# A decoder trunk on one core: value product behind the third head's q and k, gate products ahead of the z products, transposes one step later

## The chip, the cores and the metric

The kernel runs on one core of a Trainium2 chip. The metric is the device time of one launch in microseconds. Before the change three runs gave 2627.89, 2624.89 and 2626.27 us; their median is 2626.27 us.

## What is computed

Two layers of a hybrid decoder trunk over 512 tokens of width 1024, all in float32. Each layer is a half-step feed-forward block, a mixer and a second half-step feed-forward block; a last norm follows. The change touches the mixer only:

```python
proj = h @ w_in[l]
q, k, v, z, xbc, dt_raw, gate_sb, gate_ssm = jnp.split(proj, IN_SPLITS, axis=-1)
y_sb = stick_breaking_attention(q, k, v) @ w_branch_sb[l]              # 4 heads x 128
y_ssm = mamba2_mixer(z, xbc, dt_raw, ...) @ w_branch_ssm[l]            # 24 heads x 64, 8 groups
merged = jax.nn.sigmoid(gate_sb) * y_sb + jax.nn.sigmoid(gate_ssm) * y_ssm
x = x + merged @ w_out[l]
```

Inside `mamba2_mixer`, xbc goes through a causal convolution of four taps and silu and splits into x, b and c; a chunked scan over four chunks of 128 tokens gives y, which is multiplied with silu(z) and normalised by groups.

## The kernel before

Activations lie transposed, channels on the 128 partitions and the 512 tokens along the free axis. Every float32 operand of a product is kept as two parts, a rounded high part and the rest (`hhi` and `hlo` for the input h, `whi` and `wlo` for weights), and one product of a 128x128 weight block with 128x512 activations is three TensorE matmuls (`mm3`, lines 316 to 320). A weight unit is 128 output columns over 1024 inputs: one DMA of 512 KB into `wraw`, a ScalarE cast into `whi` (line 285) and a VectorE subtraction into `wlo` (line 287), two units ahead of use. A product over it is eight times `mm3`.

The order of the work on every engine is the order in which the program issues it. The main stream issues products. Beside it runs a list of generators (`spawn`): after each `mm3` of a product, `tick` lets every generator whose count has run out issue its next instructions. `yield n` in a generator means: go on n steps later. So a **step** is one `mm3` of the main stream, and the number in a yield sets how many matmuls TensorE has in front of it when it meets the generator's next instruction. TensorE takes matmuls in that order; when an operand is not there, everything behind it waits. `flush` runs the steps that are left without a product between them.

The products go round four PSUM banks of the pool `pmm` (trace name `mm`); attention's scores and the scan use `pa` (two banks), transposes and the heads' value products `ptr` (two banks, trace name `pt`). A product that writes the bank of the product four places before it needs that one read out.

Order of the mixer's products. `qkv_order` (line 105) gives q and k of heads 0 and 1, then v, then q and k of head 2, dt, and q and k of head 3. The first four are issued before the loop over the order: q0 and k0 into `pa`, q1 and k1 into two `mm` banks. During k1 the input h is replaced by its normed form, block by block (`swapped`, lines 352 to 359, `hhi` at 357 and `hlo` at 358). The four outputs q0 to k1 are scaled by the norm afterwards (`scaled`, trace name `raw`, lines 546 and 548) and split into `yt` pairs (lines 406 and 411); q and k of the later heads are split straight from PSUM. v and z are made token by token (`by_tokens`, line 877): four weight units, and in each of them all four token blocks c = 0 to 3, so all four `mm` banks are in use at once; c = 0 opens its bank at once, c = 3 opens the last one after six `mm3`. v has 512 columns, z 384, and a matmul of 384 columns takes less time. z of pair p has four units.

`attention` (line 906) runs as one generator for each head, one head at a time: scores of four key blocks (lines 929 to 943), suffix sums on TensorE and weights (lines 945 to 964, in buffers `dec`, `btok`, `cT` and `bT`, two of each, one pair for each head), and, when all weights and all of v are there (line 983), the value product into `pt` (lines 986 to 989). `opened` (line 995) holds the end of each convolution until all four heads and dt are done.

`group_steps` (line 62) orders the rest in four pairs p: b and c of two groups, three x blocks, z, and gate products (`gs`, `gm`) where a 1 or a true condition stands. `conv_block` (line 1001) reads a bank with one ScalarE and three VectorE instructions (lines 1009 and 1012), then takes tanh (1017) and one VectorE instruction (1024), yields 2, and transposes x and b on TensorE (`transposed`, line 854, trace line 859). Its two scratch tiles come from the rooms `raw` and `cv`, three of each. `sigma` (line 1214) reads a gate's bank with one tanh (1218). `z_part` (line 1050) reads z's banks (1067, 1069). `ssd_group` (line 1077) is the scan of one group, one group at a time; at its end the group's result `yn` (trace name `raw`, line 1193) and every second time `tail` (`acc`) are transposed after `yield 3`.

Of the kernel before, what the change touches and what calls it, by code (L numbers as in the profile page):

```python
# [19 lines left out]
NT = SEQ // P  # L20
# [3 lines left out]
SBH = 4  # L24
# [37 lines left out]
def group_steps():  # L62


    gates = iter([(t, m) for m in range(EARLY) for t in ("gs", "gm")])
    for p in range(GROUPS // 2):
        a, b = 2 * p, 2 * p + 1
        if p == 0:
            steps = [("z", p), ("b", a), 1, ("c", a), ("x", 0), 1, ("x", 1), ("x", 2), 1, ("b", b), ("c", b), 1]
        else:  # L70
            steps = [("b", a), ("c", a), 1, ("x", 3 * p), ("x", 3 * p + 1), ("z", p), ("x", 3 * p + 2), p < 3,
                     ("b", b), ("c", b), p < 2, p < 2]
            if p == 3:
                steps[2] = 0
        for step in steps:
            if step in (0, 1):
                if step:
                    yield next(gates)
            else:
                yield step  # L80
    yield from gates
    for m in range(EARLY, KB):
        yield "gs", m
        yield "gm", m


def conv_at(kind, i):

    if kind == "x":
        return OFF_X + i * P, i * TAPS  # L90
    at = (OFF_B, OFF_C)[kind == "c"] + i * P
    return at, (DIN // P + GROUPS * (kind == "c") + i) * TAPS
# [12 lines left out]
def qkv_order():  # L105


    yield from (("q", 0), ("k", 0), ("q", 1), ("k", 1))
    for u in range(NT):
        yield "v", u  # L110
    for h in range(2, SBH):
        yield from (("q", h), ("k", h))
        if h == SBH - 2:
            yield "dt", None


# [5 lines left out]
def unit_order(layer):  # L122
# [14 lines left out]
    for t, h in qkv_order():  # L137
        yield ((layer, "dt") if t == "dt" else (layer, t, h)), KB
    for kind, i in group_steps():
        if kind == "z":  # L140
            for u in range(NT):
                yield (layer, "z", i, u), 2 * 2 * GW // P
        else:
            yield (layer, kind, i), KB
# [22 lines left out]
class Builder:  # L167
# [833 lines left out]
    def conv_block(self, kind, i, ps):  # L1001


        nc, mp = self.nc, self.mp
        r = yield from self.take("raw")
        u = yield from self.take("cv")
        _, k0 = conv_at(kind, i)
        tap = [self.conv[:, k0 + j:k0 + j + 1] for j in range(TAPS)]
        nc.scalar.activation(u, ps, AF.Identity, scale=tap[KCONV - 1], bias=tap[KCONV])
        yield 2  # L1010
        for j in range(1, KCONV):
            nc.vector.scalar_tensor_tensor(u[:, j:], ps[:, :SEQ - j], tap[KCONV - 1 - j], u[:, j:],  # L1012
                                           op0=ALU.mult, op1=ALU.add)
            yield 1
        yield 1
        yield from self.opened()
        nc.scalar.activation(r, u, AF.Tanh)
        yield 1
        if self.cumb is None:
            self.load_cum(0)  # L1020
        dst = u
        if kind != "x":
            dst = self.ssm[i][kind] = self.t(mp, [P, SEQ], kind + "T")
        nc.vector.scalar_tensor_tensor(dst, r, 1.0, u, op0=ALU.add, op1=ALU.mult)
        yield 2
        if kind == "x":
            p, i = divmod(i, 3)
            pt = self.transposed(dst)
            yield 1
            for g in (2 * p, 2 * p + 1):  # L1030
                a, b = max(i * P, g % 2 * GW), min((i + 1) * P, (g % 2 + 1) * GW)
                if a < b:
                    if "x" not in self.ssm[g]:
                        while not self.room["xs"]:
                            yield 1
                        self.room["xs"] -= 1
                        self.ssm[g]["x"] = self.t(mp, [P, NT, GW], "xs", bufs=3)
                    nc.scalar.activation(self.ssm[g]["x"][:, :, a - g % 2 * GW:b - g % 2 * GW],
                                         pt[:, :, a - i * P:b - i * P], AF.Copy, scale=0.5)
                    self.ssm[g]["x", i] = True  # L1040
            yield 1
        elif kind == "b":
            pt = self.transposed(dst, NT - 1)
            yield 1
            tok = self.t(mp, [P, NT - 1, P], "btok")
            nc.scalar.copy(tok, pt)
            self.ssm[i]["btok"] = tok
        self.give("raw", "cv")
# [28 lines left out]
    def ssd_group(self, layer, g):  # L1077
# [120 lines left out]
        if g % 2:  # L1198
            todo.append((tail, 3 * (g // 2) + 2))
        for src, blk in todo:  # L1200
            yield 3
            pt = self.transposed(src.rearrange("p c d -> p (c d)")).rearrange("p c d -> p (c d)")
            if src is yn:
                self.give("raw")
            yield 1
            gain = par[:, G_SSM + blk:G_SSM + blk + 1]
            hi, lo = self.pair(self.yt, ("yt", "yt"))
            nc.scalar.activation(hi, pt, AF.Copy, scale=gain)
            yield 1
            nc.vector.scalar_tensor_tensor(lo, pt, gain, hi.bitcast(F32), op0=ALU.mult, op1=ALU.subtract)  # L1210
            self.y_ssm[blk] = (hi, lo)
# [31 lines left out]
    def mixer(self, layer):  # L1243
# [4 lines left out]
        self.hx = []  # L1248
        first = []
        order = list(qkv_order())  # L1250
        for i in range(4):
            while i == 3 and self.scaled_blocks < KB // 2:
# [4 lines left out]
        with ExitStack() as mix:  # L1257
# [20 lines left out]
            with tc.tile_pool(name=f"mp{layer}", bufs=2, reuse_waits="tile") as self.mp:  # L1278
# [23 lines left out]
                for kind, i in group_steps():  # L1302
                    if kind == "z":
                        self.by_tokens(partial(self.z_part, i), 2 * GW, layer, "z", i)
                    elif kind in ("gs", "gm"):
                        gates.setdefault(i, []).append(open_gate(kind, i))
                    else:
                        self.spawn(self.conv_block(kind, i, self.project(layer, kind, i)[0]))
# [197 lines left out]
```

## Time and profile before

| what | value |
|---|---|
| median of three runs | 2626.27 us |
| the profiled execution, its own time | 2627.45 us |
| its span, first to last instruction | 2625.5 us |
| mean granted TensorE clock | 0.997 |
| VectorE busy | 1748.9 us (67%) |
| ScalarE busy | 1280.8 us (49%) |
| GpSimd busy | 506.9 us (19%) |
| mixer of layer 0, first product of v to the last transposes | about 379 to 838 us |

The profile shows one execution. Times in it are microseconds from the first instruction. PE is TensorE, PEld its weight loads, DVE VectorE, ACT ScalarE, POOL GpSimd. A busy PE need not be at its peak: a matmul's record lasts longer than the distance to the next one, since they are pipelined. In the timeline a row gives start, duration, engine, line, operation, tiles as out<-in, form and count, and in brackets how long the engine was idle before it and which instruction ended that.

### The profile page before, as it was taken

The numbers are of one execution on the slowest core, as the hardware profiler recorded it, in microseconds if no ns is written. First come the engines' busy times: TensorE is split into PE (matmuls) and PEld (weight loads), VectorE is DVE, ScalarE is ACT, GpSimd is POOL, SyncE is SP. The second block draws the span as 40 slices with busy tenths as digits, with TensorE's granted clock in tenths as the row PEclk, the third lists the DMA queues.
The fourth block names the chain that finished last, engine by engine and source line by source line (L and its number), as shares of the span: only waits on it lengthen the run. The fifth ranks groups of instructions, "written<-read, shape, count | busy, mean of one in ns | idle before, by whom it ended". The sixth has DMA issues, their size and how long they took to land.

```text
span 2625.5 us, 38311 instructions
## 1 busy us (share of the span) xinstructions
PE 2588.9 (99%) x15122; PEld 2307.6 (88%) x15122; DVE 1748.9 (67%) x2362; ACT 1280.8 (49%) x2087; POOL 506.9 (19%) x629
## 2 busy tenths in 40 slices
PE   9999999999999999999999999999999999999998
PEld 7898978888888889899998989788888888899997
DVE  7575875565675478585885858656666744776766
ACT  6343556755554255353553535466555532543434
POOL 1120201133232003021120311012322310021210
PEclk9999999999999999999999999999999999999999
DMA  6465442333333555474554645323333335474642
GB/s 185 137 155 140 122 133 73 100 101 116 101 100 94 164 149 158 134 184 112 160 143 123 178 128 133 118 74 107 101 108 99 100 110 163 130 183 127 178 122 80
DMA packets 105157, 336.36 MB, mean 128 GB/s; under 512 B 12256, under 2 KB 15584, under 8 KB 104976
## 3 DMA queue, kind: packets, MB, share of 16 engines
q1 hardware_dynamic: 93168, 293.46, 35.8%
q0 software_dynamic: 10944, 39.85, 8.6%
q8 instruction: 119, 1.95, 0.3%
q10 hardware_dynamic: 864, 0.60, 0.1%
q14 instruction: 62, 0.51, 0.1%
HBM read 321.18 MB, written 12.68 MB: 127 GB/s over the span
## 4 chain that ended last, share of the span: by engine, by line
PE 90%; DVE 6%; ACT 2%; issue 1%; DMA 1%; POOL 0%; SPq 0%; DVEq 0%; ACTq 0%
PE mm L318 25%; PE mm L320 25%; PE mm L319 25%; PE pa L320 3%; PE pa L319 3%; PE pa L318 3%; DVE wlo L287 2%; PE pa L1142 1%; DVE cv L1012 1%; ACT whi L285 1%; PE pa L953 1%; PE pt L859 1%; PE pa L1144 1%; PE pt L1127 1%; PE pt L1125 0%
## 5 line engine op out<-in xcount | busy, mean ns | idle before, releaser
L285 ACT CAST whi<-wraw 128x1024 fp32r<-128x1024 f32 (+2 forms) x442 | 435.8, 986 | 601.7 <-PE mm L320 487.7
L287 DVE TENSOR_TENSOR wlo<-wraw,whi 128x1024 fp32r<-128x1024 f32 (+2 forms) x442 | 544.6, 1232 | 209.5 <-ACT whi L285 208.8
L318 PE MATMUL mm<-hhi,whi 128*128 128x512 f32 (+1 forms) x1600 | 575.0, 359 | 1.1 <-ACT hhi L505 1.1
L319 PE MATMUL mm<-hhi,wlo 128*128 128x512 f32 (+1 forms) x1600 | 559.9, 350 | 2.1 <-DVE wlo L287 2.1
L320 PE MATMUL mm<-hlo,whi 128*128 128x512 f32 (+1 forms) x1600 | 560.8, 351 | 0.1
L320 PEld LDWEIGHTS mm<-hlo,whi 128*128 128x128 f32 x1600 | 303.1, 189 | 40.9 <-DVE hlo L507 0.5
L319 PEld LDWEIGHTS mm<-hhi,wlo 128*128 128x128 f32 x1600 | 303.7, 190 | 39.1 <-DVE wlo L287 3.3
L318 PEld LDWEIGHTS mm<-hhi,whi 128*128 128x128 f32 x1600 | 303.6, 190 | 38.0 <-DVE z L1069 1.6
L622 POOL TENSOR_TENSOR g<-g,rs 128x512 f32<-128x512 f32 x76 | 132.7, 1746 | 736.0 <-DVE g L629 715.2
L318 PE MATMUL mm<-act,whi 128*128 128x512 f32 (+1 forms) x710 | 274.3, 386 | 0.0
L287 DVE TENSOR_TENSOR wlo<-s,whi 128x1024 fp32r<-128x1024 f32 x152 | 235.4, 1563 | 58.5 <-ACT whi L285 58.5
L319 PE MATMUL mm<-act,wlo 128*128 128x512 f32 (+1 forms) x710 | 274.1, 386 | 0.0
L320 PE MATMUL mm<-act,whi 128*128 128x512 f32 (+1 forms) x710 | 274.0, 386 | 0.0
L320 PE MATMUL mm<-tl,whi 128*128 128x256 f32 x912 | 258.6, 284 | 0.0
L319 PE MATMUL mm<-th,wlo 128*128 128x256 f32 x912 | 258.6, 284 | 0.0
L318 PE MATMUL mm<-th,whi 128*128 128x256 f32 x912 | 258.5, 283 | 0.0
L285 ACT CAST whi<-s 128x1024 fp32r<-128x1024 f32 x152 | 158.9, 1045 | 100.7 <-PE mm L320 59.0
L648 DVE SCALAR_TENSOR_TENSOR x<-mm,x 128x512 f32<-128x512 f32 x93 | 64.1, 690 | 196.1 <-PE mm L320 196.1
L319 PEld LDWEIGHTS mm<-th,wlo 128*128 128x128 f32 x912 | 175.3, 192 | 0.0
L318 PEld LDWEIGHTS mm<-th,whi 128*128 128x128 f32 x912 | 175.3, 192 | 0.0
L320 PEld LDWEIGHTS mm<-tl,whi 128*128 128x128 f32 x912 | 175.3, 192 | 0.0
L320 PEld LDWEIGHTS mm<-act,whi 128*128 128x128 f32 x710 | 133.5, 188 | 26.7
(288 smaller groups left out, 5036.1 us busy)
## 6 DMA issues: line engine op xcount, KB each, us to landing
wraw<-in_wflat_dram SPq DMA_DIRECT2D x330, 512.0 KB, 3.8
s<-in_wflat_dram SPq DMA_DIRECT2D x76, 512.0 KB, 5.0
s<-in_wflat_dram POOLq DMA_DIRECT2D x76, 512.0 KB, 9.2
wraw<-in_wflat_dram SPq DMA_DIRECT2D x96, 384.0 KB, 3.1
cumb<-cum_d SPq DMA_DIRECT2D x16, 768.0 KB, 4.3
xd<-x SPq DMA_DIRECT2D x16, 256.0 KB, 3.3
wraw<-in_wflat_dram SPq DMA_DIRECT2D x16, 256.0 KB, 3.1
x<-xd SPq DMA_DIRECT2D x16, 256.0 KB, 5.5
```

The source lines that it names most:

```text
L285: nc.scalar.copy(hi[:, :n], raw[:, :n])
L287: nc.vector.tensor_tensor(lo[:, :n], raw[:, :n], hi[:, :n].bitcast(F32), op=ALU.subtract)
L318: mm(ps, a[0], b[0], start=start, stop=False, **kw)
L319: mm(ps, a[1], b[0], start=False, stop=False, **kw)
L320: mm(ps, a[0], b[1], start=False, stop=stop, **kw)
L622: eng.tensor_tensor(r, r, self.rs[:, cols].unsqueeze(1).to_broadcast([P, 2, half]), op=ALU.mult)
L648: self.nc.vector.scalar_tensor_tensor(x, pd, 0.5, x, op0=ALU.mult, op1=ALU.add)
L859: self.nc.tensor.transpose(pt[:, cs], src[:, cs], self.ident)
L953: nc.tensor.matmul(pz[:, (i - j) * P:n], lhs, part, start=False, stop=(i == j and part is sps[i][1]), skip_group_check=True)
L1012: nc.vector.scalar_tensor_tensor(u[:, j:], ps[:, :SEQ - j], tap[KCONV - 1 - j], u[:, j:], op0=ALU.mult, op1=ALU.add)
L1127: nc.tensor.matmul(pu, btok[:, c, :], xws[c].rearrange("p h d -> p (h d)"), start=True, stop=True)
L1142: nc.tensor.matmul(py[:, i * HD:(i + 1) * HD], decs[c][:, i, :], xdts[c][:, i, :], start=True, stop=True)
```

## The change

Three edits. `group_steps` moves gate products: in pairs 1 and 2 one now stands just ahead of z, and the others move to other places of the pair; the number of gate products in each pair stays. `qkv_order` puts v behind q and k of head 2 and ahead of dt. Two yields grow by one: between a convolution's last VectorE instruction and its transposes, and between a group's `yn` and `tail` and their transposes. The weights in memory follow the order of the products.

```diff
         else:
-            steps = [("b", a), ("c", a), 1, ("x", 3 * p), ("x", 3 * p + 1), ("z", p), ("x", 3 * p + 2), p < 3,
-                     ("b", b), ("c", b), p < 2, p < 2]
-            if p == 3:
-                steps[2] = 0
+            steps = [("b", a), ("c", a), p < 2, ("x", 3 * p), ("x", 3 * p + 1), p < 3, ("z", p), ("x", 3 * p + 2),
+                     ("b", b), p < 3, ("c", b), p < 2]
...
-    yield from (("q", 0), ("k", 0), ("q", 1), ("k", 1))
-    for u in range(NT):
-        yield "v", u
-    for h in range(2, SBH):
+    for h in range(SBH):
         yield from (("q", h), ("k", h))
         if h == SBH - 2:
+            for u in range(NT):
+                yield "v", u
             yield "dt", None
...
         nc.vector.scalar_tensor_tensor(dst, r, 1.0, u, op0=ALU.add, op1=ALU.mult)
-        yield 2
+        yield 3
         if kind == "x":
...
         for src, blk in todo:
-            yield 3
+            yield 4
             pt = self.transposed(src.rearrange("p c d -> p (c d)")).rearrange("p c d -> p (c d)")
```

With G for a gate product, the order of the pairs before and after:

```
before  p=1: b2 c2 G x3 x4 z x5 G b3 c3 G G   p=2: b4 c4 G x6 x7 z x8 G b5 c5   p=3: b6 c6 x9 x10 z x11 b7 c7
after   p=1: b2 c2 G x3 x4 G z x5 b3 G c3 G   p=2: b4 c4 x6 x7 G z x8 b5 G c5   p=3: b6 c6 x9 x10 z x11 b7 c7
```

## The prediction

> **What bounds the kernel now.** First the page: its span, the busy line of its first part, and the chain of its fourth.
>
> ```profile
> span 2625.5 us, 38311 instructions
> PE 2588.9 (99%) x15122; PEld 2307.6 (88%) x15122; DVE 1748.9 (67%) x2362; ACT 1280.8 (49%) x2087; POOL 506.9 (19%) x629
> PE 90%; DVE 6%; ACT 2%; issue 1%; DMA 1%; POOL 0%; SPq 0%; DVEq 0%; ACTq 0%
> ```
>
> TensorE is busy 99% of the span and carries 90% of the chain that ended last. The change leaves the number and the sizes of the matmuls as they are. So it can win only what TensorE now loses by waiting, and any new wait of TensorE is paid in full. The view of waits, TensorE alone (total us, times, longest):
>
> ```profile
> PE mm L318 <- DVE cv L1012: 4.8, 6, 1.0
> PE mm L318 <- DVE raw L546: 3.8, 2, 1.9
> PE mm L318 <- DVE raw L548: 3.5, 2, 1.7
> PE pt L859 <- DVE raw L1193: 2.5, 2, 1.2
> PE pt L859 <- DVE bT L1024: 2.4, 4, 0.6
> PE pt L859 <- DVE cv L1024: 2.2, 4, 1.0
> ...
> PE pa L1142 <- DVE dec L1133: 1.3, 2, 0.7
> ```
>
> Three kinds of wait belong to the three edits: products that wait for the `raw` tiles of q1 and k1 (7.3 us, v), products that wait for a convolution's tap L1012 (4.8 us, z), transposes L859 that wait for VectorE (7.1 us). The last row belongs to none of them, and no row of the view names a DMA. Next the timeline of TensorE through v of layer 0, and where the same stretch begins and ends in layer 1:
>
> ```profile
> 379.30 0.39 PE L318 MATMUL mm<-whi,hhi 128*128 128x512 f32 x1
> ...
> 381.79 0.39 PE L320 MATMUL mm<-wlo,hhi 128*128 128x512 f32 x1
> 383.92 0.50 PE L318 MATMUL mm<-whi,hhi 128*128 128x512 f32 x1 [1.75 <-DVE raw L548]
> ...
> 387.46 0.70 PE L318 MATMUL mm<-whi,hhi 128*128 128x512 f32 x1 [1.89 <-DVE raw L546]
> ...
> 388.81 0.63 PE L318 MATMUL mm<-whi,hhi 128*128 128x512 f32 x1
> 389.24 0.63 PE L319 MATMUL mm<-whi,hlo 128*128 128x512 f32 x1
> ...
> 391.89 0.22 PE L318 MATMUL pa<-yt,yt 128*128 128x128 f32 x1
> ...
> 1679.50 0.39 PE L318 MATMUL mm<-whi,hhi 128*128 128x512 f32 x1
> ...
> 1692.12 0.22 PE L318 MATMUL pa<-yt,yt 128*128 128x128 f32 x1
> ```
>
> The twelfth matmul starts at 381.79, eleven distances after the first at 379.30: 0.226 us each. A record of 0.39 thus runs 0.16 beyond the next start, so a stop costs 0.16 more than the idle time in its bracket. Head 0's first scores come after ten steps, thirty matmuls: 6.79 us at that pace. They start 12.59 later in layer 0 and 12.62 in layer 1: **5.80 and 5.83 us lost per v**. The two stops make 1.75 + 1.89 + 2 x 0.16 = 3.96; the rest is a slower clock right behind them, 0.43 us from 388.81 to 389.24. The view of windows (us, busy and count of PE, PEld, DVE, ACT, POOL, granted clock, DMA):
>
> ```profile
> 387.60:391.00 3.40, 3.40 (x9) 2.64 (x10) 0.69 (x1) 1.50 (x2) 0.00 (x0) 0.50 0.10 42
> 1688.10:1691.50 3.40, 3.40 (x10) 2.66 (x9) 1.18 (x2) 1.21 (x2) 0.00 (x0) 0.50 0.06 19
> ```
>
> The granted clock is 0.50 for 3.4 us after v's second stop, in both layers; nine matmuls at 0.43 in place of 0.226 are 1.8 us. [...]
>
> **Part 1, v behind q2 and k2.** Removed: both stops and the slow clock. q1 and k1 keep their banks until VectorE has scaled them; v reaches those banks in its first unit, two steps of its own per bank. Afterwards q2 and k2, sixteen steps or 10.9 us, lie between, and they write the other two banks. What is late next? First h itself: q2 reads all eight blocks of the new h in eight steps, where v read two in its first unit. VectorE in that stretch:
>
> ```profile
> 377.84 1.22 DVE L287 TENSOR_TENSOR wlo<-wraw,whi 128x1024 fp32r<-128x1024 f32 x1
> 378.98 3.10 DVE L358 TENSOR_TENSOR hlo<-x,hhi 128x512 fp32r<-128x512 f32 x5
> ...
> 383.78 1.22 DVE L287 TENSOR_TENSOR wlo<-wraw,whi 128x1024 fp32r<-128x1024 f32 x1
> 384.91 1.89 DVE L411 TENSOR_TENSOR yt<-raw,yt 128x512 fp32r<-128x512 f32 x3
> ```
>
> The last five `hlo` are done at 382.08, 0.62 apart, so block 3 at 379.6. q2 would start at 379.30 and read block k's `hlo` at 379.75 + 0.68 k: block 3 at 381.8, block 7 at 384.5. Margin 2.2 us or more. The `wlo` of 377.84 serves the unit that starts at 384.74, that of 383.78 the one at 390.2. No wait. Second, head 0's scores, now after ten unbroken steps at 379.30 + 6.8 = 386.1: they read k0's low part, the second of the three L411, done at 384.91 + 2/3 x 1.89 = 386.17. A wait of 0 to 0.3 us. Third, k2's bank, which v needs three blocks into its first unit, 4.1 us after k2 ends; it is released by one ScalarE cast and one VectorE subtraction issued one and two steps after (0.6 and 0.7 us by rows like L411's): covered by 2 us, and were it not, the excess would be paid. The weight fetches behind this change places on SP's queue, but q2's, k2's and v's units are all one fetch of 512 KB, and the order of use is the order of fetching: 0.
>
> Fourth, the value products. Head 0's waits for all of v, whose last part is split two steps after step 48 instead of after step 32. It came after step 44; it will come after about step 53. Head 1 writes its own weights into the same buffer pair:
>
> ```profile
> 420.54 0.39 PE L318 MATMUL pt<-bT,yt 128*128 128x512 f32 x1
> 427.41 0.30 ACT L406 CAST dec<-cumb 128x128 fp32r<-128x128 f32 x1
> ```
>
> Twelve matmuls from 420.54 take 1.9 us. The cast to `dec` is issued at step 51, ahead of step 53 on another engine, so ScalarE will stand there some 3 us (two steps and the 1.9), with `btok`'s cast and what follows queued behind it. TensorE needs nothing of that before head 1's next scores, and the weight casts of the next two products are already done. I take 0 for it; a bound above is those 3 us per layer, if TensorE had to wait as long. **Term: -11.6, new wait 0 to 0.3 per layer** besides that bound.
>
> **Part 2, gates before z.** Part 3's stops are in the same fence, layer 0 only; layer 1 repeats them.
>
> ```profile
> 508.59 0.41 PE L859 MATMUL pt<-ident,cv 128*128 128x128 f32 x2 [0.17 <-DVE cv L1024]
> ...
> 583.16 0.44 PE L859 MATMUL pt<-ident,cv 128*128 128x128 f32 x2 [0.97 <-DVE cv L1024]
> ...
> 587.31 0.41 PE L318 MATMUL mm<-whi,hhi 128*128 128x384 f32 x1 [0.95 <-DVE cv L1012]
> 587.56 0.33 PE L319 MATMUL mm<-whi,hlo 128*128 128x384 f32 x1
> 587.73 0.33 PE L320 MATMUL mm<-wlo,hhi 128*128 128x384 f32 x1
> ...
> 632.51 0.55 PE L859 MATMUL pt<-ident,bT 128*128 128x128 f32 x3 [0.60 <-DVE bT L1024]
> ...
> 680.93 0.41 PE L318 MATMUL mm<-whi,hhi 128*128 128x384 f32 x1 [0.52 <-DVE cv L1012]
> ...
> 725.74 0.44 PE L859 MATMUL pt<-ident,bT 128*128 128x128 f32 x2 [0.60 <-DVE bT L1024]
> ...
> 757.24 0.41 PE L318 MATMUL mm<-whi,hhi 128*128 128x384 f32 x1 [0.92 <-DVE cv L1012]
> ...
> 796.92 0.52 PE L859 MATMUL pt<-ident,raw 128*128 128x128 f32 x3 [1.23 <-DVE raw L1193]
> ```
>
> z of pairs 1, 2 and 3 stops once each, at its fourth bank, 18 matmuls of 0.17 (3.1 us) after the x product that filled it. With a gate product (eight steps, 5.4 us) between, x's bank has moved to c = 2 and has 7.5 us: gone. The fourth bank now holds the gate, released by a single tanh, issued two steps after:
>
> ```profile
> 570.86 0.58 ACT L1218 ACTIVATE gs<-mm 128x512 f32<-128x512 f32 x1
> ```
>
> 0.58 us inside 3.1 leaves 1.5 us for ScalarE's queue even after the two steps. Pair 3 keeps its order and its 0.92. **Term: 2 x (0.95 + 0.52 + 2 x 0.16) = -3.6.** Against it stands that pair 2 then has four convolutions in a row; pair 3 has that today and pays one stop of 0.60.
>
> **Part 3, one step later.** A step is 0.68 us of matmuls in front of the transposes. It covers the stops of 0.17 and twice 0.60 wholly, and one of 0.11 that this view cuts off (the waits of `bT` sum to 2.4 over four in two layers); 0.97 and 1.23 shrink by 0.68 each. Per layer 0.17 + 0.11 + 0.60 + 0.60 + 0.68 + 0.68 = 2.84, and 0.16 for each of the four that vanish: 3.5. **Term: -7.0.** Cost: a block holds its two scratch tiles one step longer, some 12 steps where a product takes eight; so two blocks at most hold them at once, and there are three of each.
>
> The sum is -22.2. New stops: from 0 to the 3.6 and 7.0 of parts 2 and 3, which a shifted order on VectorE can give back; I take 1 us per layer, nearest the stops under 1 us that stand in the rows today. **-20.2 against 2627.45 of the profiled execution is 2607.2; that execution lies 1.2 above the median, so 2606.**
>
> **The rivals.**
>
> *New stops instead of the old.* At 583.16 and 796.92 VectorE was late by other work, not by few steps, and between pairs 1 and 3 every instruction moves. If all of parts 2 and 3 comes back, only v's 11.6 stays, less 2: 2615 to 2617. The many separate stops speak against losing all. 0.15.
>
> *The extra step does nothing*, because TensorE meets the same late result behind other matmuls: part 3 is 0, 2613. The stops of 0.60 were single and shorter than a step, which speaks against it. 0.09.
>
> *The slow clock stays.* [...] 0.05.
>
> *q2 waits where v waited*, for `hlo` or `wlo`: 11.6 is lost, 2618. The margin of 2.2 us speaks against it. 0.05.
>
> *Slower.* `opened` lets no convolution end before the fourth head is out. If the held head 0 pushes all heads back, convolutions keep their banks and TensorE stands:
>
> ```profile
> 505.88 1.68 ACT L1017 ACTIVATE raw<-cv 128x512 f32<-128x512 f32 x3
> ...
> 512.02 0.78 ACT L1009 ACTIVATE cv<-mm,conv 128x512 f32<-128x512 f32 x1 [0.52 <-PE mm L320]
> ```
>
> Three blocks waited for it; the fourth read its bank at 512.02 the moment its product ended, 6.1 us after, and that bank is written again only four products on (21.8 us), some 4 us of reading taken off. So lateness costs from 6.1 + 21.8 - 4 = 24 us on. To lose 22.2 + 5.3 us it must be 38 us in each layer: 2632. I find 3 us. 0.02.
>
> *Better.* The changed order also takes away the third z stop, `dec` and the halves left over: all the idle time of the three kinds and of `dec`, 2598 to 2602. 0.06.
>
> **How the numbers follow.** The forecast, 2602 to 2611, has 0.58. The range 2600 to 2618 leaves out a part of the better case, the slower one and the tail of the first and fourth rival. Less than 0.2% (5.3 us) is about what a measurement of this kernel cannot tell from no change; that needs v's gain lost together with another part, 0.05 from the first and fourth rival. Slower 0.02, faster 0.93.
>
> **What would show it.** In the profile after: no wait on `raw` L546 or L548 by `mm`, no window of half clock in the mixers, one wait on L1012 per layer, near 0.9; waits of L859 below 1 us per layer in sum. Wrong would be: `mm` waiting for `hlo` L358 in q2, a long TensorE wait beside head 1's `dec`, or new rows of L1012 and L1024 as large as the old.

## The result and the profile after

The changed kernel takes 2602.95 us (median of 4 runs, 2602.21 to 2603.63) against 2627.08 us before (4 runs, 2624.89 to 2628.09): a ratio of 0.9909, 95% interval 0.9892 to 0.9926. The forecast was 2606 in a range of 2600 to 2618. The profile page of the changed kernel, its span, busy line and chain of waits (its line numbers are three lower than before's from `conv_block` on and in the helpers: L315 is the old L318):

```profile
span 2601.4 us, 38331 instructions
PE 2581.0 (99%) x15122; PEld 2306.4 (89%) x15122; DVE 1743.4 (67%) x2362; ACT 1278.6 (49%) x2087; POOL 505.0 (19%) x629
PE 93%; DVE 4%; ACT 2%; issue 1%; DMA 1%; POOL 0%; SPq 0%; DVEq 0%; ACTq 0%
```

The matmuls are as many as before, 15122; the share of the chain on VectorE fell from 6% to 4% and that on TensorE rose from 90% to 93%. The view of waits of the changed kernel, TensorE alone (total us, times, longest):

```profile
PE mm L315 <- DVE cv L1009: 1.8, 2, 0.9
PE pt L856 <- DVE cv L1021: 1.2, 4, 0.3
...
PE pt L1122 <- DVE state L1132: 0.7, 2, 0.3
```

Both `raw` rows of v (7.3 us), the transposes' waits for `raw` and `bT`, and `dec` are gone. The taps (now L1009) keep one wait per layer in place of three. New are a wait for the scan's `state`, 0.35 per layer, and the four waits of L856 for `cv`: before, the waits for `cv` stood at 508.59 and 583.16, in the changed kernel they stand at 618.28 and 704.58.

For everything below one measure is used, since it leaves out what the rest of the program does: the time of a mixer in the one execution of each kernel that was profiled, from the first matmul of q0 to the first matmul of the branch product that follows the transposes. The timeline of TensorE has both ends; first before, layer 0:

```profile
356.62 0.39 PE L318 MATMUL pa<-hhi,whi 128*128 128x512 f32 x1
...
841.83 0.39 PE L318 MATMUL mm<-yt,whi 128*128 128x512 f32 x1
```

and the same two rows of the changed kernel:

```profile
357.18 0.39 PE L315 MATMUL pa<-hhi,whi 128*128 128x512 f32 x1
...
829.93 0.39 PE L315 MATMUL mm<-yt,whi 128*128 128x512 f32 x1
```

485.21 us became 472.75. In layer 1 it is 1656.83 to 2141.99 and 1644.89 to 2117.62: 485.16 became 472.73. So each mixer lost 12.46 and 12.43 us, 24.9 together. The span fell by 24.1: the part ahead of the first mixer took 0.56 more (356.62 against 357.18) and the rest 0.2; the first of these differs from run to run (the first mixer began between 355.9 and 358.4 in the runs below).

The stretch that v held before now holds q2 and head 0's scores. Timeline of TensorE, changed kernel:

```profile
379.85 0.39 PE L315 MATMUL mm<-hhi,whi 128*128 128x512 f32 x1
...
386.65 0.22 PE L315 MATMUL pa<-yt,yt 128*128 128x128 f32 x1
386.82 0.33 PE L316 MATMUL pa<-yt,yt 128*128 128x128 f32 x1
...
553.03 0.35 PE L1122 MATMUL pt<-cT,bT 128*128 128x128 f32 x1 [0.35 <-DVE state L1132]
...
618.28 0.41 PE L856 MATMUL pt<-ident,cv 128*128 128x128 f32 x2 [0.29 <-DVE cv L1021]
...
704.58 0.41 PE L856 MATMUL pt<-ident,cv 128*128 128x128 f32 x2 [0.30 <-DVE cv L1021]
...
746.74 0.41 PE L315 MATMUL mm<-whi,hhi 128*128 128x384 f32 x1 [0.89 <-DVE cv L1009]
```

The ten steps from 379.85 to 386.65 take 6.80 us, the pace of the prediction, without a stop. The second matmul of the scores, the first that reads k0's low part, follows after 0.17; before, the same one followed after 0.06 (391.89 to 391.95). So between 0.1 and 0.2 us is lost there. The last four rows are the stops that layer 0 has left. With 0.16 added to each as in the prediction, 0.51 + 0.45 + 0.46 + 1.05 = 2.5 us.

### The profile page after: what moved, and what is told of

Same layout as the page of the kernel before. It is cut to its first block, busy times and chain, and to the rows that moved or that the text cites. A ratio compares the mean times of both kernels' runs of the same rounds, so it can differ in the third digit from the quotient of the medians.

```text
span 2601.4 us, 38331 instructions
## 1 busy us (share of the span) xinstructions
PE 2581.0 (99%) x15122; PEld 2306.4 (89%) x15122; DVE 1743.4 (67%) x2362; ACT 1278.6 (49%) x2087; POOL 505.0 (19%) x629
## 4 chain that ended last, share of the span: by engine, by line
PE 93%; DVE 4%; ACT 2%; issue 1%; DMA 1%; POOL 0%; SPq 0%; DVEq 0%; ACTq 0%
PE mm L315 26%; PE mm L317 26%; PE mm L316 26%; PE pa L316 3%; PE pa L317 3%; PE pa L315 3%; PE pa L1139 1%; PE pt L856 1%; DVE wlo L284 1%; PE pa L950 1%; PE pa L1141 1%; PE pt L1124 1%; ACT whi L282 1%; PE pt L1122 1%; DVE cv L1009 0%
## 5 line engine op out<-in xcount | busy, mean ns | idle before, releaser
L315 PE MATMUL mm<-hhi,whi 128*128 128x512 f32 (+1 forms) x1600 | 572.3, 358 | 1.1 <-ACT hhi L502 1.1
L315 PEld LDWEIGHTS mm<-hhi,whi 128*128 128x128 f32 x1600 | 303.3, 190 | 36.9 <-ACT hhi L502 1.5
L315 PE MATMUL mm<-act,whi 128*128 128x512 f32 (+1 forms) x710 | 274.0, 386 | 0.0
L315 PE MATMUL mm<-th,whi 128*128 128x256 f32 x912 | 258.1, 283 | 0.0
L315 PEld LDWEIGHTS mm<-th,whi 128*128 128x128 f32 x912 | 175.1, 192 | 0.0
L1009 DVE SCALAR_TENSOR_TENSOR cv<-mm,conv,cv 128x511 f32<-128x511 f32 x168 | 125.0, 744 | 51.2 <-ACT cv L1006 49.7
```

The source lines that it names most:

```text
L315: mm(ps, a[0], b[0], start=start, stop=False, **kw)
```

## The experiments

The table gives each run's ratio and, by the two rows shown above, how far each of its mixers differs from 485.21 and 485.16 (us).

| kernel | ratio to before, 95% | mixer 0, change | mixer 1, change |
|---|---|---|---|
| changed kernel | 0.9909, 0.9892 to 0.9926 | -12.46 | -12.43 |
| e1, v alone | 0.9961, 0.9947 to 0.9975 | -5.64 | -5.63 |
| e2, gates alone | 0.9998, 0.9989 to 1.0007 | -1.62 | +0.08 |
| e3, both yields alone | 0.9954, 0.9941 to 0.9968 | -5.26 | -6.82 |
| e9, the convolution's yield alone | 0.9954, 0.9939 to 0.9969 | -6.88 | -6.86 |
| e10, the group's yield alone | 0.9973, 0.9963 to 0.9983 | -3.64 | -3.59 |
| e4, k1 in a tile of another room | 0.9975, 0.9965 to 0.9985 | -3.72 | -3.70 |
| e8, v and both yields, no gates | 0.9923, 0.9906 to 0.9939 | -10.91 | -10.91 |
| e5, a gate ahead of the last z too | 0.9907, 0.9892 to 0.9922 | -13.52 | -13.56 |
| e6, e5 with one gate less behind pair 1 | 0.9906, 0.9891 to 0.9920 | -13.52 | -13.43 |
| e7, both yields one more | 0.9917, 0.9902 to 0.9932 | -12.08 | -11.74 |

A difference here also holds the half clock of before for each mixer in which it is absent. By the view of windows it is present in both mixers of e10 and in mixer 1 of e2, and absent in mixer 0 of e2 although v's stops stand there (rows in the last section): e2's two mixers, with one edit, differ by 1.70 us. For e3 and e9 no view shows the clock there, and it is estimated from the times: e3's mixers differ by 1.56, so mixer 0 is taken to have the half clock and mixer 1 not, and neither mixer of e9: they gain as much as that mixer 1 (6.88 and 6.86 against 6.82), with idle time in the view of waits near e3's (5.7 us at the taps and `dec` against 6.1 at the taps and `state`, both layers).

### e1, v alone

```diff
-    yield from (("q", 0), ("k", 0), ("q", 1), ("k", 1))
-    for u in range(NT):
-        yield "v", u
-    for h in range(2, SBH):
+    for h in range(SBH):
         yield from (("q", h), ("k", h))
         if h == SBH - 2:
+            for u in range(NT):
+                yield "v", u
             yield "dt", None
```

> The kernel before with v alone moved behind q2 and k2. Theory (the parts add up): the stops on raw L546 and L548 and both half-clock windows are gone, 11.6 us, against at most 0.3 us of new wait per layer: 11 to 11.6 us less, and the z and transpose stops stay as they are (4.8 and 7.1 us of idle time in the view of waits). Rival (the edits work only together, since VectorE and ScalarE have less slack when TensorE no longer pauses): new stops later in the mixer give part of it back, 6 to 9 us less. Rival (q2 waits for the new h in place of v): under 3 us less.

Measured: 2616.48 us, 9.8 less than the 2626.28 beside it; per mixer 5.64 and 5.63 less, 11.3 together. Of the 1.5 between the two figures, 0.9 is the part ahead of the first mixer (it began at 357.54 in e1, at 356.62 before), and 0.6 is the distance of the two profiled executions from their medians. Both stops are gone, and by the time so is the half clock, since 5.64 is 1.68 more than the 3.96 of the stops; all the waits of the other two kinds stand as before (its rows, one line number lower):

```profile
PE mm L317 <- DVE cv L1011: 4.8, 6, 0.9
...
PE pt L858 <- DVE raw L1192: 2.5, 2, 1.2
PE pt L858 <- DVE bT L1023: 2.4, 4, 0.6
PE pt L858 <- DVE cv L1023: 2.2, 4, 1.0
PE pa L1141 <- DVE dec L1132: 1.3, 2, 0.7
```

So v's move and the rest do not touch each other.

### e2, gates alone

```diff
-            steps = [("b", a), ("c", a), 1, ("x", 3 * p), ("x", 3 * p + 1), ("z", p), ("x", 3 * p + 2), p < 3,
-                     ("b", b), ("c", b), p < 2, p < 2]
-            if p == 3:
-                steps[2] = 0
+            steps = [("b", a), ("c", a), p < 2, ("x", 3 * p), ("x", 3 * p + 1), p < 3, ("z", p), ("x", 3 * p + 2),
+                     ("b", b), p < 3, ("c", b), p < 2]
```

> The kernel before with the gate products alone moved. Theory (parts add up): the z stops of pairs 1 and 2 go (0.95 and 0.52 us per layer, 0.16 us more for each), pair 3 keeps its 0.92: 3.6 us less. If the four convolutions in a row of pair 2 make VectorE late, new stops of 0.5 to 1 us per layer appear and 1.5 to 2.5 us less remain. If the gates also take the stop at the dec tiles (0.66) away, 5.4 us less.

Measured: 2626.5 us, no change. The view of waits of e2 (two lines lower than before), and one row of its timeline:

```profile
PE pt L857 <- DVE raw L1191: 6.7, 6, 1.2
...
PE mm L316 <- DVE cv L1010: 1.8, 2, 0.9
```

```profile
624.34 0.33 PE L857 MATMUL pt<-ident,raw 128*128 128x128 f32 x1 [1.06 <-DVE raw L1191]
```

The z stops of pairs 1 and 2 left as predicted: six waits on the tap fell to two, 4.8 to 1.8 us. But the transposes of a group's `yn` now wait six times in place of two, 6.7 in place of 2.5 us. The moved gates changed which instructions stand side by side, and a convolution's taps fell ahead of `yn` on VectorE. Timeline of VectorE in e2:

```profile
622.16 1.52 DVE L1010 SCALAR_TENSOR_TENSOR cv<-mm,conv,cv 128x510 f32<-128x510 f32 x2
623.60 0.68 DVE L1191 TENSOR_TENSOR raw<-y,gny 128x512 f32<-128x512 f32 x1
```

Two taps, 1.52 us, end just before `yn` starts at 623.60; TensorE meets its transpose 1.06 us early, and again at 712.61 by 1.04. In the kernel before, the same `yn` follows the norm's last small instruction (L495) with no tap between, and the next tap comes 4 us later:

```profile
623.45 0.16 DVE L495 SCALAR_TENSOR_TENSOR gny<-gnt,gny 128x4 f32<-128x4 f32 x1
623.72 0.69 DVE L1193 TENSOR_TENSOR raw<-y,gny 128x512 f32<-128x512 f32 x1
627.02 0.75 DVE L1210 SCALAR_TENSOR_TENSOR yt<-pt,par,yt 128x512 fp32r<-128x512 f32 x1 [2.61 <-ACT yt L1208]
627.69 0.74 DVE L1012 SCALAR_TENSOR_TENSOR cv<-mm,conv,cv 128x511 f32<-128x511 f32 x1
```

The prediction's rival, new stops in place of the old, is what happens to this part when it stands alone. The 1.62 of mixer 0 is not the gates' doing: that mixer of e2 has no half clock, and mixer 1, which has it, differs by 0.08 (rows in the last section).

### e3, both yields alone

```diff
-        yield 2
+        yield 3
         if kind == "x":
...
-            yield 3
+            yield 4
             pt = self.transposed(src.rearrange("p c d -> p (c d)")).rearrange("p c d -> p (c d)")
```

> The kernel before with the transposes alone one step later. Theory (a step is 0.68 us of cover): stops of 0.17, 0.11 and twice 0.60 us go, those of 0.97 and 1.23 shrink by 0.68: 7.0 us less. Rival (the stops that are longer than a step come from other work on VectorE that the extra step also moves): they vanish wholly, 8 to 9 us less. Rival (TensorE meets the same late result): 0 to 3 us less.

Measured: 2614.61 us, 11.7 less, where the prediction's term was 7.0. The view of waits of e3 (lines as before):

```profile
PE mm L318 <- DVE cv L1012: 5.4, 6, 1.3
...
PE pt L1125 <- DVE state L1135: 0.7, 2, 0.3
```

No transpose L859 waits any more, though two of the stops were 0.97 and 1.23, longer than the 0.68 of a step, and `dec` (1.3) went with them. Cover alone can't do that. VectorE before, ahead of the transposes that stopped at 796.92:

```profile
794.65 1.52 DVE L1012 SCALAR_TENSOR_TENSOR cv<-mm,conv,cv 128x510 f32<-128x510 f32 x2
796.10 0.68 DVE L1193 TENSOR_TENSOR raw<-y,gny 128x512 f32<-128x512 f32 x1
```

and the same place in e3:

```profile
787.31 0.74 DVE L1012 SCALAR_TENSOR_TENSOR cv<-mm,conv,cv 128x510 f32<-128x510 f32 x1
...
790.27 0.74 DVE L1012 SCALAR_TENSOR_TENSOR cv<-mm,conv,cv 128x509 f32<-128x509 f32 x1
790.93 0.69 DVE L1193 TENSOR_TENSOR raw<-y,gny 128x512 f32<-128x512 f32 x1
```

Before, two taps stood between the norm's small instructions and `yn`; in e3 one of them came earlier, at 787.31, ahead of those. A yield that grows by one moves the generator's later VectorE work as well as the transposes, so `yn` is ready a tap sooner (0.74) and is asked for a step later (0.68): 1.42 together, more than 1.23. At the stop of 0.97 two instructions changed places. Before, the convolution's last one (L1024) stood behind `yn`:

```profile
581.81 0.69 DVE L1193 TENSOR_TENSOR raw<-y,gny 128x512 f32<-128x512 f32 x1
582.42 0.69 DVE L1024 SCALAR_TENSOR_TENSOR cv<-raw,cv 128x512 f32<-128x512 f32 x1
```

and in e3 it stands ahead of it:

```profile
579.60 0.69 DVE L1024 SCALAR_TENSOR_TENSOR cv<-raw,cv 128x512 f32<-128x512 f32 x1
580.21 0.68 DVE L1193 TENSOR_TENSOR raw<-y,gny 128x512 f32<-128x512 f32 x1
```

That is 0.61 sooner, and the step that covers it lies in a z product, whose steps take three times 0.17, 0.5 us: 1.1 together, more than 0.97.

The rows do not give all of e3's gain. In layer 0 the view's stops that went make 5.2 us with 0.16 for each, and `state` (0.51) and the first z stop, which grew from 0.95 to 1.26, take 0.8 of it back: 4.4 of the measured 5.26. Of the other 0.9, 0.1 is the stop at a `bT` transpose that the prediction counted and the view cuts off; where the rest went stays open.

### e9 and e10, one yield each

```diff
-        yield 2
+        yield 3
         if kind == "x":
```

> The kernel before with only the convolutions' transposes one step later (yield 3), the groups' as before. Both yields together took 9.5 us of stops away, more than the 7.0 predicted: the stops at dec (0.66) and at raw (1.23) went wholly, and the first z stop grew by 0.3. Theory (a later x block starts a group's scan one step later, and so moves the scan's VectorE instructions past the convolutions'): dec and raw go here as well, with all of bT and cv: 9 to 11 us less than the kernel before. Rival (they went because of the group's own later transposes): raw's 1.23 and dec's 0.66 stay, 4 to 6 us less.

```diff
         for src, blk in todo:
-            yield 3
+            yield 4
```

> The kernel before with only the groups' transposes one step later (yield 4). Theory (cover of one step, nothing else moves): raw's stop of 1.23 shrinks to 0.55, bT and cv stay: 1.4 us less than the kernel before. Rival (this yield is what removed raw and dec): 4 to 5 us less. Both are near what the clock alone does, 1.8 us for a window at half clock that may be there or not, so the stops in the trace decide.

Measured: 2613.79 and 2619.71 us beside 2626.14. The waits of e9, the convolution's yield:

```profile
PE mm L318 <- DVE cv L1012: 5.3, 6, 1.3
...
PE pa L1142 <- DVE dec L1133: 0.4, 2, 0.2
```

and of e10, the group's yield:

```profile
PE mm L318 <- DVE cv L1012: 3.7, 6, 0.9
...
PE pt L859 <- DVE cv L1024: 2.3, 4, 1.0
...
PE pt L859 <- DVE raw L1193: 1.1, 2, 0.6
```

By cover alone e10 could only shorten the two stops on `raw`, and it does so by a step (2.5 to 1.1 over two layers). But the four stops on `bT` (2.4) and both on `dec` (1.3) went too, and the taps' waits fell from 4.8 to 3.7. Neither `bT` nor `dec` is behind the yield that was changed, so this is order and not cover: before, the group's L1210 ran on VectorE at 627.02, ahead of a tap at 627.69 (rows under e2); in e10 a tap comes first and L1210 behind it:

```profile
623.38 0.75 DVE L1012 SCALAR_TENSOR_TENSOR cv<-mm,conv,cv 128x511 f32<-128x511 f32 x1 [1.08 <-ACT cv L1009]
...
625.46 0.75 DVE L1210 SCALAR_TENSOR_TENSOR yt<-pt,par,yt 128x512 fp32r<-128x512 f32 x1
```

Per layer, cover took 0.67 off the stop on `raw`; the stops on `bT` (1.52 with 0.16 for each), on `dec` (0.82) and the shorter first z stop (0.53) make 2.9. e9 takes off nearly all that e3 does, only 0.19 per layer stays on `dec`: the two yields reach the same stops by different ways and their gains overlap, not add.

### e4, one stop of v alone

```diff
-    def qkv_parts(self, t, ps, normed, parts):
+    def qkv_parts(self, t, ps, normed, parts, room="raw"):
...
-        r = yield from self.take("raw")
+        r = yield from self.take(room)
...
-        self.give("raw")
+        self.give(room)
...
-                    self.spawn(self.qkv_parts(t, ps, normed, parts[h]))
+                    self.spawn(self.qkv_parts(t, ps, normed, parts[h], "cv" if (t, h) == ("k", 1) else "raw"))
```

> The kernel before, with k1's scaled output in a tile of the cv room, so that its scaling no longer waits for a raw tile to come free: v keeps its first stop (1.75 us) and loses its second (1.89). Theory (half clock needs both stops within a few us): no window of half clock, 2.05 + 1.8 us less per layer, 7 to 8 us less in all. Rival (one stop, or v's place, is enough for half clock): the half-clock windows stay, 4 us less. [...]

v stays where it was, but k1's scaled form needs no `raw` tile and so doesn't wait for q0, q1 or k0 to give one back. Measured: 2619.92 us beside 2626.28, and 3.72 and 3.70 less per mixer. The first stop stands:

```profile
PE mm L318 <- DVE raw L548: 3.5, 2, 1.7
```

The second is gone. The stop is worth 1.89 + 0.16 = 2.05; what remains of 3.70, 1.65, is near the 1.70 between e2's two mixers and is put down to the half clock, an estimate: the one stretch of e4 whose clock a view shows, 383.02 to 386.43, has 1.00. So in e4, with v in its old place and the first stop alone, the price of the slow clock is not paid. Whether the second alone would bring it, no run shows.

### e8, the change without its gates

```diff
-            steps = [("b", a), ("c", a), p < 2, ("x", 3 * p), ("x", 3 * p + 1), p < 3, ("z", p), ("x", 3 * p + 2),
-                     ("b", b), p < 3, ("c", b), p < 2]
+            steps = [("b", a), ("c", a), 1, ("x", 3 * p), ("x", 3 * p + 1), ("z", p), ("x", 3 * p + 2), p < 3,
+                     ("b", b), ("c", b), p < 2, p < 2]
+            if p == 3:
+                steps[2] = 0
```

> The changed kernel with the gate products put back to their old places (v moved, transposes later). Moved alone the gates changed nothing. Theory (they pay only where the transposes come a step later): the z stops of pairs 1 and 2 are back, 1.5 and 0.7 us per layer with the ends of the records, and 0.8 us of small stops of the changed kernel go: 2 to 3 us slower than the changed kernel, 2605 to 2606. Rival (the gates are worth nothing in any surrounding): 2603.

Measured: 2605.04 us; per mixer 10.91 less. e1 and e3 give 5.64 + 5.26 = 10.90 for layer 0, where e3 is taken to have the half clock as before has it: v and the yields then add. The waits of e8:

```profile
PE mm L317 <- DVE cv L1011: 5.3, 6, 1.3
...
PE pt L1124 <- DVE state L1134: 0.7, 2, 0.4
```

From here to the changed kernel the gates take the taps' 5.3 to 1.8 and bring 1.2 for the convolutions' transposes: 2.3 us of idle time over both layers, 1.15 each. The mixers differ by more, 12.46 - 10.91 = 1.55 each; the remaining 0.4 is in no row of this view. The waits at the convolutions' transposes are new here: neither e3 nor e8 has any, so they come with the gates. So the gates, worth nothing alone, are worth 1.55 per layer once the transposes come later, since the stops at `yn` that e2 showed don't arise: the wait for `raw` is absent from the changed kernel's view. The ratios of the two kernels, with intervals that overlap, can't tell this difference; the mixers can.

### e5 and e6, the last z too

e5, from the changed kernel:

```diff
-            steps = [("b", a), ("c", a), p < 2, ("x", 3 * p), ("x", 3 * p + 1), p < 3, ("z", p), ("x", 3 * p + 2),
+            steps = [("b", a), ("c", a), p < 2, ("x", 3 * p), ("x", 3 * p + 1), 1, ("z", p), ("x", 3 * p + 2),
```

> The changed kernel with a gate product ahead of the last z too, taken from the six behind pair 3. Theory (the last z stop has the same cause as the others, and the scan's last steps do not need the sixth gate product as cover): 1.06 us per layer less, 2.1 us less than the changed kernel, about 2601. Rival (with one product less behind c7 the last group's steps run without matmuls between and TensorE waits for its yn): the stop goes, but 1 to 4 us per layer come at L856, the same or up to 6 us slower.

e6 is e5 with one gate taken from the end of pair 1:

```diff
-                     ("b", b), p < 3, ("c", b), p < 2]
+                     ("b", b), p < 3, ("c", b), 0]
```

> As e5, but the gate product is taken from the end of pair 1, so that six remain behind pair 3. Theory: the last z stop goes, and five convolutions in a row (c3 b4 c4 x6 x7) cost new stops of 0 to 1 us per layer: the same to 2.1 us less than the changed kernel. Rival (convolutions in a row make VectorE late by more than a gate saves): 1 to 3 us slower.

Measured: 2601.12 and 2600.52 us beside 2625.33. The mixers are 1.06 shorter in e5 than the changed kernel's in layer 0 (471.69 against 472.75). The last z stop, 0.89 + 0.16, is gone, and the view of e5 has one more wait at a convolution's transposes, 0.29 + 0.16 (six of L856, 1.7 in all, for four, 1.2). The rows thus give 0.60; as in e8, the other 0.4 or so is in no row. The gate that pair 3 now takes was to be issued later anyway, and no other new wait stands in the view. e6 is the lowest time of all, but its interval and the changed kernel's lie upon each other; 1.06 per layer is under what the ratios can tell.

### e7, another step

```diff
-        yield 3
+        yield 4
         if kind == "x":
...
-            yield 4
+            yield 5
```

> The changed kernel with both kinds of transposes one more step later (yields of 4 and 5). Theory (each step is 0.68 us of cover): the two stops of 0.51 us per layer at a convolution's transposes go, 2 us less than the changed kernel. Rival (a step moves the group's chain as well, and what is saved at the transposes returns at the next bank or in the scan): within 1 us, with new rows of z or of the scan in the view of waits.

Measured: 2603.75 us, and the mixers are longer than the changed kernel's by 0.38 and 0.69. The waits of e7:

```profile
PE pt L1122 <- DVE state L1132: 1.9, 2, 1.1
...
PE mm L315 <- DVE z L1066: 1.1, 4, 0.3
```

The stops at the convolutions' transposes went (no row of L856), but the one on `state` grew from 0.35 to 0.77 in layer 0 and 1.09 in layer 1, and z's own reading is late four times. More cover is no gain here: the delay moves on to the next instruction that needs the group.

## Why the prediction was right, and where it was not

Per layer the prediction summed 5.8 for v, 1.8 for the gates and 3.5 for the transposes, less 1.0 for new waits: 10.1. Measured: 12.45. The waits it named, the direction and the range held; two of its terms and the last step of its sum did not.

**v.** Measured 5.63 alone, for a term of 5.8 less 0 to 0.3. Both stops and the half clock went (the granted clock is 1.00 in every window of 0.5 us of the changed kernel's two mixers); q2 found h and its weights; k0's low part cost 0.1 to 0.2. That head 0's value product would hold ScalarE some 3 us at head 1's `dec` is in the trace of the changed kernel:

```profile
424.27 0.30 ACT L403 CAST dec<-cumb 128x128 fp32r<-128x128 f32 x1 [3.75 <-PE pt L316]
```

It stood 3.75 us, and no stop of TensorE is near it, so 0 was right. The rivals *q2 waits*, *slow clock stays* and *slower* fell here.

**Gates.** The z stops of pairs 1 and 2 went, and pair 3's stayed at 0.89 (said 0.92). The two stops were worth more than the 1.8 said: without the gates they measure 1.25 and 0.52 (e8), since the later transposes lengthen the first. The step that failed is that the term stood by itself: alone it is worth 0 (e2), in the whole change 1.55 for 1.8 (e8). The 1.55 has the two new waits at the convolutions' transposes taken off. What the first rival feared for parts 2 and 3 together is true of this part without the other.

**Transposes.** The term was mis-sized: 5.26 in place of 3.5 per layer (e3, mixer 0, taken to have the clock of before). Two steps failed. That 0.97 and 1.23 "shrink by 0.68 each": they went whole, because VectorE's order moved. And that `dec`, the row that "belongs to none of them", would stay: it went with the group's yield (e10) and shrank from 0.66 to 0.19 with the convolution's (e9). About 0.9 of the 5.26 is in no row. The rival *the extra step does nothing* fell. The convolution's yield suffices for it: e9's 6.87, taken to be without the half clock, is 5.2 when the 1.70 us of that clock in e2 are taken off, an estimate.

**New waits.** 1.0 per layer was taken off, a choice within bounds and not a count. Measured: `state`, 0.51 with the 0.16, which e3 has too, and the two waits of L856, 0.29 and 0.30, 0.91 with 0.16 for each, which come with the gates: 1.4. Their own sum, 0.6, is below 1 as said. So the size was near, but no single one of them was foreseen.

In the 5.26 and the 1.55 these new waits are taken off already. Before that, the transposes are worth 5.77 for 3.5 and the gates 2.46 for 1.8. The differences of the four terms, -0.17 for v, +0.66 for the gates, +2.27 for the transposes and -0.42 for the new waits, make 2.34, and 12.45 - 10.1 is 2.35.

**The last step.** From 2607.2 the prediction went to 2606, because the profiled execution lay 1.2 above the median. That carries the 1.2 over to the changed kernel, and there it is not found: its profiled execution, 2603.14, lies 0.2 above its median. From profile to profile the forecast was off by 4.1, and that the median came within 3.1 is in part luck. A likely reason, not shown since one execution of each kernel has a trace: the profiled execution of before has both half clocks, and others have fewer. In the executions of before that were timed beside the runs the granted clock is 0.996 or 0.997 where they took 2626.5 to 2628.3 us, and 0.998 where they took 2624.0 to 2626.6.

## What to carry to other kernels

In an order that is written by counting steps, a number in a yield does two things: it sets how much work covers a result, and it moves every later instruction of that generator in the queues of the other engines. Price the first by the length of a step, but look up in the trace of the producing engine what stands between the last input and the result, since the second can be worth more: in e10 0.67 us per layer by the first and 2.9 by the second. Edits that take away stops of one engine need not add: v and the yields did (e8), the gates did not (e2). So try them alone and together, and expect a removed stop to come back at the next instruction whose operand is no earlier than it was: in e7 the stop on `state` grew from 0.35 to 0.77 and 1.09 us.

## What the runs showed of the hardware

The granted clock of TensorE fell to 0.50 at v's second stop in some mixers and not in others. In before, that stop ends at 387.46 in layer 0, after 1.89 us idle, and at 1687.66 in layer 1, after 1.87; the half clock begins at 387.59 and 1688.07 and lasts 3.4 us. In e10 it begins at 387.02 and 1684.08. The four begins are read from the granted clock in windows of 0.5 us; in the rest of the two mixers of before these windows show 1.00, those on the edges of the half clock apart.

In e2 TensorE has the same two stops. The row that ends the second of them in layer 0, and rows of the view of windows (us, busy and count of PE, PEld, DVE, ACT, POOL, granted clock, DMA), two of layer 0 and one of layer 1:

```profile
389.24 0.50 PE L316 MATMUL mm<-whi,hhi 128*128 128x512 f32 x1 [1.88 <-DVE raw L544]
```

```profile
387.46:390.88 3.42, 1.64 (x7) 1.37 (x8) 2.42 (x4) 0.76 (x2) 0.00 (x0) 1.00 0.48 153
390.88:394.29 3.41, 3.41 (x20) 2.91 (x19) 1.52 (x2) 2.38 (x6) 0.28 (x1) 1.00 0.14 10
...
1687.95:1691.35 3.40, 3.40 (x9) 2.66 (x10) 0.69 (x1) 1.49 (x2) 0.00 (x0) 0.50 0.11 43
```

Layer 0 has 1.00 from 387.46 to 394.29, in the stop and behind it; layer 1 has 0.50 from 1687.95 to 1691.35. Mixer 0 is 1.62 us shorter than in before and mixer 1 0.08 longer, so here the half clock is worth 1.70 us; the nine slow matmuls of the prediction make 1.8. Why it comes in one mixer and not in the other is not shown: the second stop is 1.88 us where it stays away, and 1.89 and 1.87 where it comes in before. All of it is from one profiled execution of each kernel.
